# Differential attention on one core: the values' product in split form for two query tiles at once, and another order of the steps of a tile

## The chip, the cores and the metric

One Trainium2 chip, one core of it. The metric is the device time of one execution in microseconds (us), the median of the runs shown. The whole program is one launch: a hybrid layer (a state space part and forgetting attention), then a second block with differential and dilated attention, a projection and a gate. The change concerns the differential attention of the second block alone, which takes some 350 us of the 2730.

## The reference, cut to what matters

Four heads, 1024 queries and keys. Each head has two score matrices (`c`), whose softmaxes are combined with one factor `lam` and multiplied with the values of width 128.

```python
def diff_attention(q, k, v, lam, slopes):
    """q, k: (B,S,H,2,Dh) normalised; v: (B,S,H,2Dh). Returns (B,S,H,2Dh)."""
    ...
    def block(args):
        qblk, qp = args
        s = jnp.einsum('bqhce,bkhce->bchqk', qblk, k).astype(jnp.float32) * scale
        dist = jnp.abs(qp[:, None] - pos[None, :]).astype(jnp.float32)
        s = s - slopes[:, None, None] * dist
        a = jax.nn.softmax(s, axis=-1)
        w = a[:, 0] - lam * a[:, 1]
        return jnp.einsum('bhqk,bkhe->bqhe', w.astype(v.dtype), v)
```

## The kernel before

All data are float32. A product that must be accurate is made in one of two forms. The split form (`mm3`, lines 112 to 114) takes each operand as a rounded part "hi" of type fp32r and a rest "lo", and makes three matmuls: hi by hi, hi by lo, lo by hi. The plain form gives TensorE float32 operands; such a matmul stands in the trace as two records.

`diff_attend` (line 1179) works through one head in eight tiles of 128 queries. For tile i:

- **A(i)**: `scores` (line 1162) for both score matrices: four matmuls of 128x512 each into a double PSUM bank (`bank2`, two of them in all, so that one A(i) fills both), then on VectorE (DVE) a reduction that adds the distance bias and finds the minimum (line 1173, one per matrix), and on ScalarE (ACT) the exponential (line 1176), which also sums the row.
- **pre(i)**: three DVE instructions that work out the factor and combine the two matrices into one, 128x1024 (lines 1193 to 1195).
- **B(i)**: eight TensorE transposes of the combined tile (line 624), four into each of two PSUM banks (`bank`, four of them in all), and two ACT copies into the tile `pt` (line 630).
- **C(i)**: the product with the values (line 1211): eight plain matmuls of 128 columns each, 16 records, into a quarter of an output bank. After four tiles ACT copies that bank to `y`.

`pipeline` (line 523) writes the order out: A(0), A(1), and then for each i: pre(i), A(i+2), C(i-1), B(i). Engines work in the order in which their instructions are written, and wait for each other by semaphores.

`merge` puts work of the next head between these steps, by a count of estimated times and the factor `RATIOS[0]`: pieces of twelve `mm3` matmuls of the next head's k projection (called S below) and the steps of `pair_finish` for the head before. Its small sums are transposed by the lines 264 and 271, and it ends with a product over the whole head on DVE (line 1156). When the loop reaches tile 6 it gives `None`: from there on `pair_project` calls the remaining steps between its own (the `t` in `ORDERS`), which are the next head's other projections and the normalisation of q and k (`N`, with the lines 255, 264, 271 again). The values of a head, transposed to have tokens on partitions (`vtok`, line 469), are made at the end of `pair_project`.

Names below: K is the least time from the start of one tile's transposes to the start of the next tile's, if only the chain of waits counts.

Of the kernel before, what the change touches and what calls it, by code (L numbers as in the profile page):

```python
# [9 lines left out]
F32 = mybir.dt.float32  # L10
F32R = mybir.dt.float32r
BF16 = mybir.dt.bfloat16
I32 = mybir.dt.int32
AF = mybir.ActivationFunctionType
ALU = mybir.AluOpType
# [51 lines left out]
class Kern:  # L67
# [389 lines left out]
            self.nc.sync.dma_start(out=st[0][o:p, :n].bitcast(F32), in_=st[1][a:b, :n].bitcast(F32))  # L457
            self.nc.sync.dma_start(out=st[1][o:p, :n].bitcast(F32), in_=st[0][a:b, :n].bitcast(F32))

    def v_tokens(self, vT, blocks):  # L460

        nc = self.nc
        v = self.slot("vtok", w=1024)
        vv = v.rearrange("p (b c) -> p b c", c=128)
        for g in range(0, len(blocks), 4):
            ps = self.bank()
            for n, c0 in enumerate(blocks[g:g + 4]):
                nc.tensor.transpose(ps[:, n * 128:(n + 1) * 128], vT[:, c0:c0 + 128], self.ident)
            nc.scalar.activation(out=v[:, g * 128:g * 128 + 512], in_=ps, func=AF.Copy)
        return vv  # L470

    def v_meta(self, vT):

# [139 lines left out]
        yield from self.pipeline(8, A, B, C)  # L613
        nc.sync.dma_start(out=self.d_yatt[p], in_=y)

    def transposes(self, N, off, nb, pts, act=False):

        nc = self.nc
        for g in range(0, nb, 4):
            n = min(4, nb - g)  # L620
            ps = self.bank()
            for b in range(n):
                c = off + (g + b) * 128
                nc.tensor.transpose(ps[:, b * 128:(b + 1) * 128], N[:, c:c + 128], self.ident)  # L624
            self.evac(pts[g // 4][:, :n], ps[:, :n * 128].rearrange("p (b c) -> p b c", c=128), act)

    def evac(self, out, ps, act=False):
        self.ev = getattr(self, "ev", 0) + 1
# [486 lines left out]

    def v_by_tokens(self, n, st):
        vT = st.pop("vT")
        st["v"] = self.v_tokens(vT, [128 * b for b in range(8)])
        if n >= 4:
            st["vx"] = self.v_more(vT)  # L1120
            next(st["vx"])
        yield
# [56 lines left out]
    def diff_attend(self, p, st):  # L1179
        nc, te, V = self.nc, self.nc.tensor, self.nc.vector  # L1180
        y = st["y"] = self.slot("yd", w=T)
        Ws, PTs, O = {}, {}, [None]

        def A(i):
            l = self.sm.tile([128, 4], F32, tag="ld", name="ld", bufs=3)
            l0 = self.lall[:, p, i:i + 1]
            P = [self.scores(st, j, i, self.dist, DIFF_SLOPES[p], l[:, 1:2] if j else l0) for j in range(2)]
            Ws[i] = (P, l, l0)
            return 8 * 216

        def pre(i):
            P, l, l0 = Ws.pop(i)
            V.reciprocal(out=l[:, 1:2], in_=l[:, 1:2])
            V.scalar_tensor_tensor(out=l[:, 1:2], in0=l[:, 1:2], scalar=self.nlam, in1=l0, op0=ALU.mult, op1=ALU.mult)
            V.scalar_tensor_tensor(out=P[0], in0=P[1], scalar=l[:, 1:2], in1=P[0], op0=ALU.mult, op1=ALU.add)
            Ws[i] = P

        def B(i):
            P = Ws.pop(i)
            pt = self.slot("pt", w=1024)  # L1200
            r = pt.rearrange("p (b c) -> p b c", c=128)
            self.transposes(P[0], 0, 8, [r[:, :4], r[:, 4:]], act=True)
            PTs[i] = pt
            return 8 * 109

        def C(i):
            pt = PTs.pop(i)
            if i % 4 == 0:
                O[0] = self.bank()
            for b in range(8):  # L1210
                te.matmul(O[0][:, (i % 4) * 128:(i % 4 + 1) * 128], st["v"][:, b, :], pt[:, b * 128:(b + 1) * 128],
                          start=b == 0, stop=b == 7)
            if i % 4 == 3:
                nc.scalar.activation(out=y[:, (i - 3) * 128:(i + 1) * 128], in_=O[0], func=AF.Copy)
            return 8 * 218

        yield from self.pipeline(8, A, B, C, pre)

    def v_more(self, vT):

# [593 lines left out]
```

## Time and profile before

| what | us |
|---|---|
| median of 3 runs (2728.5 to 2733.69) | 2733.47 |
| the profiled execution, its own time | 2729.51 |
| its span | 2727.7 |
| TensorE (PE) busy in it | 2659.8 (98%) |
| DVE busy | 1372.3 (50%) |
| ACT busy | 1165.6 (43%) |
| GpSimd (POOL) busy | 684.5 (25%) |

The span is the time from the first to the last instruction. A matmul's record is longer than the time by which it delays the next one, since matmuls overlap in the array; so the distance from one start to the next is what a matmul costs, and a busy share of 98% says only that there is hardly a moment without one under way. A line of the timeline has the start, the duration, the engine, the line of the code, what is written from what, and in brackets how long the engine had been idle and for whom.

### The profile page before, as it was taken

The page shows a single profiled execution, that of the slowest core. Times are in us where ns is not written, and L with a number is a line of the kernel's source. Part 1 is how long each engine was busy: PE and PEld are TensorE (multiplying, and loading weights), DVE is VectorE, ACT ScalarE, POOL GpSimd, SP SyncE. Part 2 cuts the span into 40 slices and gives each one's busy share as a digit, 9 for nine tenths or more (in the row PEclk, how much of TensorE's full clock was granted, in tenths as well). Part 3 has the DMA queues.
Part 4 walks back from the last instruction along what each step waited for, and adds up shares of the span by engine and source line. Part 5 has one row for each costly group of instructions (what it writes and reads, how often), then busy time and mean ns, then how long its engine had stood idle before and what let it go on. Part 6 is the DMA issues. An engine that isn't in the chain of part 4 may idle for free. (4 is left out here: it accounts for less than half of the span.)

```text
span 2727.7 us, 38674 instructions
## 1 busy us (share of the span) xinstructions
PE 2659.8 (98%) x14925; PEld 2232.2 (82%) x14925; DVE 1372.3 (50%) x2761; ACT 1165.6 (43%) x2080; POOL 684.5 (25%) x764
## 2 busy tenths in 40 slices
PE   8999999999999999999999999999999999998999
PEld 6888888888989889889877887878877877777877
DVE  5433322233574573654756777444654555446332
ACT  5554444445343433443432123445644555445331
POOL 1112121111243342342432333111111121204321
PEclk9999999999999999999999999999999999998999
DMA  3122222221123123122168653340222223324422
GB/s 131 58 64 72 78 79 71 78 64 62 39 88 114 55 78 116 55 103 91 55 207 279 205 182 131 128 121 30 72 70 70 79 94 94 86 72 146 160 65 70
DMA packets 85464, 266.87 MB, mean 98 GB/s; under 512 B 10880, under 2 KB 12032, under 8 KB 84256
## 3 DMA queue, kind: packets, MB, share of 16 engines
q1 hardware_dynamic: 85280, 264.40, 30.3%
q8 instruction: 117, 1.92, 0.3%
q14 instruction: 67, 0.55, 0.1%
HBM read 205.57 MB, written 33.49 MB: 88 GB/s over the span
## 5 line engine op out<-in xcount | busy, mean ns | idle before, releaser
L121 POOL TENSOR_TENSOR wlo<-wraw,whi 128x1024 fp32r<-128x1024 f32 (+2 forms) x168 | 374.4, 2232 | 1288.7 <-ACT whi L120 1077.8
L112 PE MATMUL bank<-uh,whi 128*128 128x512 f32 (+4 forms) x1752 | 625.8, 357 | 0.1
L114 PE MATMUL bank<-uh,wlo 128*128 128x512 f32 (+4 forms) x1752 | 618.8, 353 | 0.1
L113 PE MATMUL bank<-ul,whi 128*128 128x512 f32 (+4 forms) x1752 | 618.5, 353 | 0.0
L114 PEld LDWEIGHTS bank<-uh,wlo 128*128 128x128 f32 (+1 forms) x1752 | 327.9, 187 | 35.4 <-POOL wlo L121 0.5
L112 PEld LDWEIGHTS bank<-uh,whi 128*128 128x128 f32 (+1 forms) x1752 | 328.3, 187 | 34.3 <-issue 1.1
L113 PEld LDWEIGHTS bank<-ul,whi 128*128 128x128 f32 (+1 forms) x1752 | 328.2, 187 | 32.3
L112 PE MATMUL bank<-u,whi 128*128 128x512 f32 x512 | 207.8, 406 | 0.7 <-ACT pr L935 0.7
L113 PE MATMUL bank<-u,whi 128*128 128x512 f32 x512 | 203.6, 398 | 0.0
L114 PE MATMUL bank<-u,wlo 128*128 128x512 f32 x512 | 203.3, 397 | 0.0
L120 ACT ACTIVATE whi<-wraw 128x1024 fp32r<-128x1024 f32 (+2 forms) x169 | 155.3, 926 | 20.5 <-DMA wraw<-in_w_pa_dram 18.2
L630 ACT ACTIVATE pt<-bank 128x512 f32<-128x512 f32 (+1 forms) x320 | 143.0, 509 | 44.8 <-PE bank L624 38.1
L114 PE MATMUL bank<-yh,wlo 128*128 128x512 f32 x384 | 152.5, 397 | 1.0 <-POOL wlo L121 0.8
L112 PE MATMUL bank<-yh,whi 128*128 128x512 f32 x384 | 152.3, 397 | 0.9 <-ACT whi L120 0.9
L113 PE MATMUL bank<-yl,whi 128*128 128x512 f32 x384 | 151.9, 395 | 0.0
L647 DVE SCALAR_TENSOR_TENSOR acc<-raw,cwh,acc 128x1040 f32<-128x1040 f32 x72 | 93.7, 1302 | 109.5 <-ACT acc L644 107.8
L573 ACT ACTIVATE N<-N,mn 128x272 f32<-128x272 f32 (+7 forms) x128 | 100.3, 786 | 45.2 <-DVE mn L570 44.0
L114 PEld LDWEIGHTS bank<-u,wlo 128*128 128x128 f32 x512 | 97.2, 190 | 23.2
L112 PEld LDWEIGHTS bank<-u,whi 128*128 128x128 f32 x512 | 97.8, 191 | 22.3 <-ACT pr L935 1.1
L113 PEld LDWEIGHTS bank<-u,whi 128*128 128x128 f32 x512 | 97.6, 191 | 20.7
L121 POOL TENSOR_TENSOR wo<-wl,wo 128x512 fp32r<-128x512 f32 x52 | 73.4, 1425 | 157.8 <-ACT wo L120 150.6
L624 PE MATMUL bank<-cm,N 128*128 128x128 f32 x832 | 106.9, 273 | 0.0
(326 smaller groups left out, 4961.5 us busy)
## 6 DMA issues: line engine op xcount, KB each, us to landing
wraw<-in_w_in_dram SPq DMA_DIRECT2D x120, 512.0 KB, 4.1
gt<-d_gate SPq DMA_DIRECT2D x48, 512.0 KB, 5.7
ab<-d_acs SPq DMA_DIRECT2D x32, 512.0 KB, 3.5
qs<-qt SPq DMA_DIRECT2D x48, 256.0 KB, 2.9
wl<-in_w_out_dram SPq DMA_DIRECT2D x48, 256.0 KB, 5.4
tab<-in_tab_dram SPq DMA_DIRECT2D x8, 1056.0 KB, 5.9
cb<-d_csp SPq DMA_DIRECT2D x16, 520.0 KB, 7.6
d_gate<-gt SPq DMA_DIRECT2D x16, 512.0 KB, 2.9
```

The lines of the kernel that those rows point to most:

```text
L112: te.matmul(ps, lh, rh, start=start, stop=False)
L113: te.matmul(ps, lh, rl, start=False, stop=False)
L114: te.matmul(ps, ll, rh, start=False, stop=stop)
L120: self.nc.scalar.activation(out=hi, in_=src, func=AF.Copy)
L121: (self.nc.vector if vector else self.nc.gpsimd).tensor_tensor(out=lo, in0=src, in1=hi.bitcast(F32), op=ALU.subtract)
L573: nc.scalar.activation(out=N[:, :W], in_=N[:, :W], func=AF.Exp, scale=-1.0, bias=mn[:, n - 1:n], accum_out=self.lall[:, 2 * p + j, i:i + 1])
L624: nc.tensor.transpose(ps[:, b * 128:(b + 1) * 128], N[:, c:c + 128], self.ident)
L630: self.nc.scalar.activation(out=out, in_=ps, func=AF.Copy)
L647: V.scalar_tensor_tensor(out=acc[:, :L], in0=raw[:, k:k + L], scalar=w(k), in1=acc[:, :L], op0=ALU.mult, op1=ALU.add)
```

## The change

The product C is made in the split form, for two tiles (256 queries) at once: 8 key blocks by 3 matmuls of 256 columns, 24 records for two tiles, where 32 stood. For this B writes hi by the ACT copy and lo by a new DVE subtraction that reads the PSUM bank and hi (two per tile), and the values get a lo of their own (two DVE subtractions per head, for the differential heads alone). The tile `pt` now holds hi and lo of both tiles of a pair, half of the keys each; it comes from a pool of its own with two buffers, so one pair fills both.

The loop is written out in place of `pipeline`: A(0), A(1), pre(0), and then for each i: B(i), A(i+2), pre(i+1), C(i-1), where C of an even tile does nothing. `None` is given ahead of B(6).

```diff
-    def v_tokens(self, vT, blocks):
+    def v_tokens(self, vT, blocks, split=False):
...
+            c = slice(g * 128, g * 128 + 512)
+            nc.scalar.activation(out=v[:, c], in_=ps, func=AF.Copy)
+            if split:
+                nc.vector.tensor_tensor(out=vs[1][:, c], in0=ps, in1=v[:, c].bitcast(F32), op=ALU.subtract)
...
+            x, hi = ps[:, :n * 128].rearrange("p (b c) -> p b c", c=128), pts[g // 4][:, :n]
+            self.evac(hi, x, act)
+            if los:
+                nc.vector.tensor_tensor(out=los[g // 4][:, :n], in0=x, in1=hi.bitcast(F32), op=ALU.subtract)
...
         def B(i):
             P = Ws.pop(i)
-            pt = self.slot("pt", w=1024)
-            r = pt.rearrange("p (b c) -> p b c", c=128)
-            self.transposes(P[0], 0, 8, [r[:, :4], r[:, 4:]], act=True)
-            PTs[i] = pt
+            if i % 2 == 0:
+                PTs[i // 2] = [self.ph.tile([128, 2, 4, 256], F32R, tag="pt", name="pt", bufs=2) for _ in range(2)]
+            q = slice((i % 2) * 128, (i % 2 + 1) * 128)
+            hi, lo = ([pt[:, x, :, q] for pt in PTs[i // 2]] for x in range(2))
+            self.transposes(P[0], 0, 8, hi, True, lo)
             return 8 * 109
 
         def C(i):
-            pt = PTs.pop(i)
-            if i % 4 == 0:
+            if i % 2 == 0:
+                return 0
+            pt, h = PTs.pop(i // 2), i // 2 % 2
+            if h == 0:
                 O[0] = self.bank()
+            o = O[0][:, h * 256:h * 256 + 256]
             for b in range(8):
-                te.matmul(O[0][:, (i % 4) * 128:(i % 4 + 1) * 128], st["v"][:, b, :], pt[:, b * 128:(b + 1) * 128],
-                          start=b == 0, stop=b == 7)
-            if i % 4 == 3:
+                hi, lo = (pt[b // 4][:, x] for x in range(2))
+                v = [x[:, b, :] for x in st["v"]]
+                self.mm3(o, v[0], v[1], hi[:, b % 4], lo[:, b % 4], b == 0, b == 7)
+            if h:
                 nc.scalar.activation(out=y[:, (i - 3) * 128:(i + 1) * 128], in_=O[0], func=AF.Copy)
-            return 8 * 218
-
-        yield from self.pipeline(8, A, B, C, pre)
+            return 8 * 357
+
+        yield A(0)
+        yield A(1)
+        pre(0)
+        for i in range(8):
+            if i == 6:
+                yield None
+            yield B(i)
+            if i + 2 < 8:
+                yield A(i + 2)
+            if i + 1 < 8:
+                pre(i + 1)
+            if i:
+                yield C(i - 1)
+        yield C(7)
```

TensorE's order in the middle of the first head, before: the transposes of tile 3 (line 624, `N_16160`), the scores of tile 6 (line 1171), the product of tile 3 (line 1211) and the transposes of tile 4.

```order
L624 MATMUL bank<-cm,N_16160 128x128 x8
L1171 MATMUL bank_16319<-qs_15924,qs_15957 128x512
L1171 MATMUL bank_16319<-qt_15925,qs_15957 128x512
L1171 MATMUL bank_16319<-qs_15924,qs_15957 128x512
L1171 MATMUL bank_16319<-qt_15925,qs_15957 128x512
L1171 MATMUL bank_16328<-qs_15926,qs_15959 128x512
L1171 MATMUL bank_16328<-qt_15927,qs_15959 128x512
L1171 MATMUL bank_16328<-qs_15926,qs_15959 128x512
L1171 MATMUL bank_16328<-qt_15927,qs_15959 128x512
L1211 MATMUL bank<-pt_16300,vtok_16034 128x128 x8
L624 MATMUL bank<-cm,N_16217 128x128 x8
```

The same place now: the transposes of tile 4 (line 629, `N_16231`), the scores of tile 6 (line 1179), and the first two matmuls of the product for the tiles 2 and 3, of 256 columns each.

```order
L629 MATMUL bank<-cm,N_16231 128x128 x8
L1179 MATMUL bank_16346<-qs_15924,qs_15957 128x512
L1179 MATMUL bank_16346<-qt_15925,qs_15957 128x512
L1179 MATMUL bank_16346<-qs_15924,qs_15957 128x512
L1179 MATMUL bank_16346<-qt_15925,qs_15957 128x512
L1179 MATMUL bank_16355<-qs_15926,qs_15959 128x512
L1179 MATMUL bank_16355<-qt_15927,qs_15959 128x512
L1179 MATMUL bank_16355<-qs_15926,qs_15959 128x512
L1179 MATMUL bank_16355<-qt_15927,qs_15959 128x512
L112 MATMUL bank<-pt,vtok_16034 128x256
L113 MATMUL bank<-pt,vtok_16034 128x256
```

The transposes of tile 4 stood behind the scores of tile 6, and stand ahead of them now; the product that follows the scores of tile 6 is that of a whole pair, and there is none behind those of tile 7.

DVE's order at the same place, before: the combination of tile 4 (`N_16217`), the two reductions of tile 6, and the combination of tile 5 (`N_16274`).

```order
L1193 RECIPROCAL ld<-ld 128x1
L1194 SCALAR_TENSOR_TENSOR ld<-ld,nlam,lall 128x1
L1195 SCALAR_TENSOR_TENSOR N_16217<-N_16226,ld,N_16217 128x1024
L1173 ISA N_16317,mn<-dist,bank_16319 128x1024
L1173 ISA mn 128x1
L1173 ISA N_16326,mn<-dist,bank_16328 128x1024
L1173 ISA mn 128x1
L1193 RECIPROCAL ld<-ld 128x1
L1194 SCALAR_TENSOR_TENSOR ld<-ld,nlam,lall 128x1
L1195 SCALAR_TENSOR_TENSOR N_16274<-N_16283,ld,N_16274 128x1024
```

And now: the same instructions with new line numbers (`N_16231` is tile 4, `N_16306` tile 5), and the subtractions of line 633, two for tile 4 and two for tile 5.

```order
L1203 SCALAR_TENSOR_TENSOR N_16231<-N_16240,ld,N_16231 128x1024
L633 TENSOR_TENSOR pt<-bank,pt 128x4x128 x2
L1181 ISA N_16344,mn<-dist,bank_16346 128x1024
L1181 ISA mn 128x1
L1181 ISA N_16353,mn<-dist,bank_16355 128x1024
L1181 ISA mn 128x1
L1201 RECIPROCAL ld<-ld 128x1
L1202 SCALAR_TENSOR_TENSOR ld<-ld,nlam,lall 128x1
L1203 SCALAR_TENSOR_TENSOR N_16306<-N_16315,ld,N_16306 128x1024
L633 TENSOR_TENSOR pt<-bank,pt 128x4x128 x2
```

On DVE nothing has changed its place; the two subtractions of a tile have come between its combination and the reductions of the tile two further on.

## Rows read from the trace of the kernel before

**Rows 1.** The page: span, TensorE's busy time, its granted clock by slices.

```profile
span 2727.7 us, 38674 instructions
PE 2659.8 (98%) x14925; PEld 2232.2 (82%) x14925; DVE 1372.3 (50%) x2761; ACT 1165.6 (43%) x2080; POOL 684.5 (25%) x764
PEclk9999999999999999999999999999999999998999
```

**Rows 2.** Busy time by engine in the differential stage (us, busy, records, clock, DMA).

```profile
1834.00:2182.00 348.00, 338.14 (x1874) 277.48 (x1873) 186.90 (x336) 182.25 (x301) 49.59 (x54) 1.00 0.23 66
```

**Rows 3.** Timeline of TensorE in the second head, tiles without work between.

```profile
1959.13 0.48 PE L1171 MATMUL bank<-qs,qs 128*128 128x512 f32 x1
...
1961.08 1.95 PE L1211 MATMUL bank<-pt,vtok 128*128 128x128 f32 x16
1962.86 1.04 PE L624 MATMUL bank<-cm,N 128*128 128x128 f32 x8
1963.65 0.48 PE L1171 MATMUL bank<-qs,qs 128*128 128x512 f32 x1
...
1964.68 0.39 PE L1171 MATMUL bank<-qs,qs 128*128 128x512 f32 x1
```

**Rows 4.** Timeline of DVE there: two reductions and a combination.

```profile
1964.88 1.22 DVE L1173 CUSTOM_DVE_ANT_0 N<-dist,bank 128x1024 f32<-128x1024 f32 x1 [0.52 <-PE bank L1171]
...
1967.17 0.16 DVE L1193 RECIPROCAL ld<-ld 128x1 f32<-128x1 f32 x1
...
1967.62 1.28 DVE L1195 SCALAR_TENSOR_TENSOR N<-N,ld,N 128x1024 f32<-128x1024 f32 x1
```

**Rows 5.** Timeline of ACT there: the two copies of a tile's transposes.

```profile
1959.49 1.06 ACT L630 ACTIVATE pt<-bank 128x512 f32<-128x512 f32 x2
```

**Rows 6.** DVE groups by shape: operations from a PSUM bank and SBUF, 128x512.

```profile
L520 DVE SCALAR_TENSOR_TENSOR zs<-zs,bank 128x512 f32<-128x512 f32 x32 | 21.6, 685 | 85.7 <-ACT zs L519 85.6
L903 DVE SCALAR_TENSOR_TENSOR gt<-gt,bank 128x512 f32<-128x512 f32 x80 | 54.4, 680 | 22.6 <-PE bank L114 22.5
```

**Rows 7.** Timeline of all engines at the start of the first head.

```profile
1841.83 0.39 PE L1171 MATMUL bank<-qs,qs 128*128 128x512 f32 x1
...
1844.11 0.08 DVE L1173 DVE_READ_ACCUMULATOR2_ANT mn<- 128x1 f32 x1
...
1844.24 0.50 PE L1171 MATMUL bank<-qs,qs 128*128 128x512 f32 x1 [0.38 <-DVE mn L1173]
...
1846.45 0.40 PE L112 MATMUL bank<-u,whi 128*128 128x512 f32 x1
...
1849.23 1.04 PE L624 MATMUL bank<-cm,N 128*128 128x128 f32 x8
```

**Rows 8.** TensorE's waits in the stage (us in total, times, longest).

```profile
PE bank L271 <- DVE rsv L246: 4.4, 3, 1.5
PE bank L271 <- POOL lall L1145: 2.7, 3, 0.9
PE bank L1267 <- DVE zs L520: 2.0, 1, 2.0
```

**Rows 9.** Timeline of DVE in the second head: line 1156 ahead of a combination.

```profile
1950.79 1.22 DVE L1156 TENSOR_TENSOR yd<-yd,rb 128x1024 f32<-128x1024 f32 x1
1951.92 0.16 DVE L1193 RECIPROCAL ld<-ld 128x1 f32<-128x1 f32 x1
```

**Rows 10.** Timeline of matmuls and weight loads in split form, 272 columns.

```profile
21.75 0.29 PE L112 MATMUL bank<-uh,whi 128*128 128x272 f32 x1
...
23.64 0.29 PE L112 MATMUL bank<-uh,whi 128*128 128x272 f32 x1
...
21.76 0.19 PEld L113 LDWEIGHTS bank<-ul,whi 128*128 128x128 f32 x1
21.88 0.19 PEld L114 LDWEIGHTS bank<-uh,wlo 128*128 128x128 f32 x1
```

**Rows 11.** Stretches behind the stage (columns as in group 2; the clock ahead of DMA).

```profile
2191.00:2194.50 3.50, 1.46 (x12) 1.11 (x11) 3.28 (x3) 2.94 (x5) 2.42 (x1) 1.00 0.45 98
2194.60:2197.90 3.30, 2.97 (x10) 2.52 (x10) 1.69 (x7) 0.96 (x2) 3.29 (x16) 0.50 0.99 330
2198.00:2201.00 3.00, 3.00 (x14) 1.92 (x14) 0.41 (x2) 1.91 (x3) 1.47 (x3) 1.00 0.08 29
2491.60:2498.30 6.70, 6.00 (x33) 5.09 (x34) 3.77 (x15) 2.41 (x6) 3.96 (x4) 0.50 0.67 238
```

More of the change, by code (lines that the diff above doesn't have):

```diff
@@ L458, in move_k @@
             self.nc.sync.dma_start(out=st[1][o:p, :n].bitcast(F32), in_=st[0][a:b, :n].bitcast(F32))
-    def v_tokens(self, vT, blocks):
+    def v_tokens(self, vT, blocks, split=False):
         nc = self.nc
-        v = self.slot("vtok", w=1024)
-        vv = v.rearrange("p (b c) -> p b c", c=128)
+        vs = [self.slot("vtok", F32R if split else F32, 1024) for _ in range(1 + split)]
+        v = vs[0]
         for g in range(0, len(blocks), 4):
@@ L468, in v_tokens @@
                 nc.tensor.transpose(ps[:, n * 128:(n + 1) * 128], vT[:, c0:c0 + 128], self.ident)
-            nc.scalar.activation(out=v[:, g * 128:g * 128 + 512], in_=ps, func=AF.Copy)
-        return vv
+            c = slice(g * 128, g * 128 + 512)
+            nc.scalar.activation(out=v[:, c], in_=ps, func=AF.Copy)
+            if split:
+                nc.vector.tensor_tensor(out=vs[1][:, c], in0=ps, in1=v[:, c].bitcast(F32), op=ALU.subtract)
+        vs = [x.rearrange("p (b c) -> p b c", c=128) for x in vs]
+        return vs if split else vs[0]
     def v_meta(self, vT):
@@ L614, in fox_attend, with transposes @@
         nc.sync.dma_start(out=self.d_yatt[p], in_=y)
-    def transposes(self, N, off, nb, pts, act=False):
+    def transposes(self, N, off, nb, pts, act=False, los=None):
         nc = self.nc
@@ L624, in transposes @@
                 nc.tensor.transpose(ps[:, b * 128:(b + 1) * 128], N[:, c:c + 128], self.ident)
-            self.evac(pts[g // 4][:, :n], ps[:, :n * 128].rearrange("p (b c) -> p b c", c=128), act)
+            x, hi = ps[:, :n * 128].rearrange("p (b c) -> p b c", c=128), pts[g // 4][:, :n]
+            self.evac(hi, x, act)
+            if los:
+                nc.vector.tensor_tensor(out=los[g // 4][:, :n], in0=x, in1=hi.bitcast(F32), op=ALU.subtract)
     def evac(self, out, ps, act=False):
@@ L1117, in v_by_tokens @@
         vT = st.pop("vT")
-        st["v"] = self.v_tokens(vT, [128 * b for b in range(8)])
+        st["v"] = self.v_tokens(vT, [128 * b for b in range(8)], n < 4)
         if n >= 4:
```

## The prediction

> **What bounds the kernel now.** I read the page first, then the stage's sums, then the timeline of single tiles. The page shows TensorE busy nearly all the time, and its clock granted in full but for one slice [rows 1]; in the differential stage too it is busy 338 of 348 us, while DVE and ACT have some 185 us of work each [rows 2]. In the timeline the reader is to see that TensorE goes from tile to tile without a break: scores from 1959.13 to 1961.08 (1.95 us), product to 1962.86 (1.78), transposes to 1963.65 (0.79), so 4.52 us a tile [rows 3]. DVE needs two reductions, 2.29 us from the first's start at 1964.88 to the reciprocal at 1967.17, and 1.73 more until the combination ends at 1967.62 + 1.28 = 1968.90 [rows 4]: about 4.0 us a tile. TensorE is the bound, but DVE is close behind, and the chain from one to the other is long. What keeps it harmless is the order: between the scores whose reductions end a combination's wait and that tile's transposes stand the scores of a further tile and a product.
>
> **What the product saves.** Plain form: 1.78 us a tile, 3.57 a pair [rows 3]. Split form with 256 columns has no row; the nearest has 272: from 21.75 to 23.64 there are 15 matmuls, 0.126 us each [rows 10], which for 256 columns is 0.119 by length (0.126 if length did not count), so 24 make 2.84 us (3.02). Saved: 0.73 us a pair, 16 pairs, **11.7 us** (8.8 at the other end). Here a rule speaks against the change: a load of weights could fail to hide behind the matmul in front. In these rows each matmul has a load of its own, recorded as 0.19 us [rows 10], and still they start 0.126 apart; were loads and matmuls to take turns, a pair would take 24 x (0.19 + 0.119) = 7.4 us. The Trainium skill, "TensorE: Matmul & The Clock Gate", section "The mechanism", says that a load overlaps running matmuls only where it goes to another group of rows, and these go to the same; by its section "LDWEIGHTS (loading the stationary operand)" a load of 128 columns takes 107 ns, and a pair would then take, as an estimate, 24 x (0.107 + 0.107) = 5.1 us. I follow the row.
>
> **What DVE gets.** Two subtractions from a bank a tile: 0.68 us each [rows 6], 0.62 when one follows another (the overlap of 0.07 that the combination shows). The shape is that of the rows, so I take it as it stands. 64 of them are 40 us, and the eight for the values 5 us more. The latter cost nothing: they only delay the first reductions of a head, and the first combination waits for the second tile's reductions anyway, a stretch of TensorE work later; without that cover, 1.2 us a head. The ACT copies remain 64, no DMA is issued or moved, and POOL's and SP's queues hold what they held.
>
> **What the order costs.** B(i) now stands ahead of A(i+2), so B(i+1) follows A(i+2) directly or with one piece between, and its combination is queued on DVE behind the two subtractions of tile i and the reductions of tile i+2. K, from the start of B(i): four transposes 0.44, 0.20 until the next engine starts (the second matrix's first matmul starts at 1964.68, so the first matrix's are issued, and DVE starts on them at 1964.88 [rows 3, 4]), two copies 1.06 [rows 5], which brings the second subtraction's start to 1.83 behind the first; its 0.62 to 2.45; reductions 2.29, combination 1.73, 0.05 back to TensorE (DVE's 1844.11 + 0.08 to 1844.24 [rows 7]): **K = 6.5 us**. TensorE's own work from B(i) to B(i+1) is 0.79 + 1.95 = 2.74, plus a piece S of 2.78 where there is one (1846.45 to 1849.23 [rows 7]), plus 2.84 for a product.
>
> By the order of the first head, TensorE waits:
> - ahead of B(0) and of B(1): the scores in front of each follow a piece S, so from their start half of them 0.93, then 0.20 + 2.29 + 1.73 + 0.05 = 5.2 us, less the 1.86 of the scores: 3.3 each;
> - ahead of B(2), with S between: 6.5 - 5.5 = 1.0;
> - ahead of B(4), with nothing between but A(5): 6.5 - 2.7 = 3.8.
>
> **The buffers.** B(2) writes the next pair's `pt`, and both buffers are held by the pair whose product C(1) stands behind A(4) on TensorE. So ACT's copies of B(2) wait for that product, and behind them on DVE the subtractions, the reductions of tile 4 and the combination of tile 3, for which B(3) waits. From the product's start: its second half frees the second buffer at 2.84, + 0.20, copy 0.57, subtraction 0.62, reductions 2.29, combination 1.73, 0.05 = 8.3 us, less the product itself 2.84: TensorE waits 5.5 us ahead of B(3), and the same ahead of B(5). For B(6) the wait is hidden by the projection that `pair_project` puts there, 24 matmuls (5.6 us).
>
> A head then waits 3.3 + 3.3 + 1.0 + 5.5 + 3.8 + 5.5 = 22.4 us; in the other three line 1156 comes ahead of the combination of tile 3 with 1.13 us [rows 9], 23.5. Four heads: **93.0 us**. What goes: the wait where A(2) followed A(1), 1841.83 to 1846.45 being 4.62 us for 3.72 of scores, 0.9 a head [rows 7], and the waits of line 271 for POOL, 2.7 in three heads [rows 8], covered by the longer stops: -6.3. What comes behind the loop: line 271's wait for DVE (4.4 in three heads [rows 8]) grows, since the transposes of tile 7 no longer stand between 264 and 271 (0.8) and the subtractions of tile 7 stand ahead of its DVE work (1.2): +2.0 in three heads and 0.8 in the last, +6.8.
>
> Sum without the clock: 93.0 - 6.3 + 6.8 - 11.7 = **+81.8 us**.
>
> **The clock.** Now the clock is full in the stage [rows 2], where the longest stop is 1.5 us [rows 8]. Behind the stage line 1267 waits 2.0 us [rows 8], until 2194.4, and from 2194.6 for 3.3 us the clock is 0.50, that is 1.2 GHz of 2.4, and full again at 2198; one stretch at half clock is 6.7 us long [rows 11]. The new order has 20 stops of 3.3 us and more in the loops and 3 of about 3.5 behind them. A stretch of 3.4 us at half clock delays TensorE by 1.7; if each stop brings one, 39 us. Some of that falls into the stops themselves, or on work that the chain of waits does not pass through. With no row for stops so long I take half, 19 us, and keep 0 and 39 as bounds.
>
> **Sum:** 81.8 + 19 = 101 us on the profiled execution's 2729.5: **2830 us**. The median of the runs shown is 4 us above that execution; a difference of 0.2%, some 5 us, is about what can be told from no change.
>
> **The rivals.**
> 1. The stops cost no clock: 2729.5 + 81.8 = 2811. For it: stops of 2 us behind the stage do not all show in the page's slices [rows 1]. Against: [rows 11].
> 2. Every stop costs the full 1.7, or longer stretches: 2811 + 39 = 2850 and above.
> 3. The buffers do not bind, as the product frees them early enough. Then ahead of B(3) TensorE has 2.74 + 2.78 + 2.84 = 8.4 of work for a K of 6.5, no wait, and ahead of B(5) 6.5 - 5.6 = 0.9: four heads lose 4 x (5.5 + 4.6) + 3.4 = 44 less, so 2767, with some clock 2780. Against it: the pool has two buffers and a pair takes both.
> 4. TensorE stays the bound, and the product's gain is all that counts: 2729.5 - 11.7 = 2718, faster. This needs K below TensorE's mean of 2.74 + 1.42 = 4.2 us a tile, thus reductions and subtractions that cost some 2.3 us less than their rows, or overlap of neighbouring tiles that DVE's order rules out. For it: DVE's mean load in the stage, 187 of 348 us [rows 2], leaves room for 45 more.
> 5. Loads and matmuls take turns: 16 x (7.4 - 2.84) = 73 us more than the sum, less what vanishes in the stops that a longer product shortens, around 2880. The Trainium skill's rule above would bring this; the trace disagrees at 272 columns [rows 10].
>
> **How the numbers follow.** Chances: forecast 0.50, rival 1 0.25, rival 2 0.12, rival 3 0.06, rival 4 0.04, rival 5 0.03. The first three are one mechanism with the clock's price open: 2811 to 2850, and some 15 us on either side for K, of which each 0.2 us moves 24 waits by 5 us: 2795 to 2865. That leaves out the rivals 3 to 5 and the far end of 2. Slower 0.95, same 0.01, faster 0.04.
>
> **What the profile after would show.** TensorE's waits headed by the transposes (line 629) waiting for DVE's combination (line 1203), 24 of them, the longest near 5.5 us ahead of the odd tiles 3 and 5; ACT's copies into `pt` of tiles 2 and 4 waiting for the product; matmuls of 256 columns some 0.119 us apart; the stage some 100 us longer, and half clock in it. The prediction is wrong if the transposes wait for nothing, if the copies of tile 2 run before the product of the first pair, or if DVE's subtractions take far less or more than 0.68 us.

## The result, and the profile after

| what | before | after |
|---|---|---|
| median, us | 2732.98 (2728.5 to 2733.69) | 2852.39 (2849.97 to 2855.56) |
| ratio, 95% interval | | 1.0444 (1.0433 to 1.0455) |
| the profiled execution, its own time | 2729.51 | 2851.41 |

Six runs of each kernel. The change makes the kernel 4.4% slower; the profiled execution is 121.9 us longer. The page of after, with the rows that answer to [rows 1], and two groups of instructions (busy time and mean ns of one, then the idle time of the engine in front of them and what ended it):

```profile
span 2849.6 us, 38478 instructions
PE 2689.1 (94%) x14797; PEld 2250.5 (79%) x14797; DVE 1418.8 (50%) x2833; ACT 1171.5 (41%) x2080; POOL 680.7 (24%) x764
PEclk9999999999999999999999999989889899999999
L629 PE MATMUL bank<-cm,N 128*128 128x128 f32 x832 | 123.1, 299 | 87.5 <-DVE N L1203 87.5
L633 DVE TENSOR_TENSOR pt<-bank,pt 128x512 fp32r<-128x512 f32 x64 | 43.7, 690 | 147.9 <-ACT pt L638 147.9
```

TensorE is recorded as busy for 29 us longer than before, although it has 128 matmuls fewer: its records are longer at half clock (one of 512 columns lasts 0.63 us there, and 0.39 at full clock). The transposes (line 629) now have 87.5 us of idle time in front of them, all ended by the combination (line 1203). TensorE's waits in the differential stage say the same, beside [rows 8]:

```profile
PE bank L629 <- DVE N L1203: 87.5, 24, 6.6
PE bank L271 <- DVE rsv L246: 7.7, 3, 2.6
PE bank L112 <- DVE pt L633: 1.6, 3, 0.5
PE bank L264 <- ACT sums L257: 1.2, 1, 1.2
```

The waits for POOL are gone. The stage and two pieces of it (columns as in [rows 2], the clock ahead of the DMA share):

```profile
1834.00:2304.00 470.00, 371.10 (x1740) 298.68 (x1739) 233.79 (x408) 187.84 (x302) 46.89 (x54) 0.88 0.17 49
1846.00:1853.00 7.00, 5.97 (x18) 5.08 (x19) 2.35 (x3) 1.79 (x4) 0.00 (x0) 0.52 0.00 0
1877.00:1883.50 6.50, 3.16 (x12) 2.90 (x13) 4.37 (x9) 4.55 (x8) 0.00 (x0) 0.50 0.01 3
```

Where the granted clock of the whole stage was 1.00, it is 0.88, so half clock (1.2 GHz) held for (1 - 0.88) x 2 x 470 = 113 us. The two pieces lie around the stops ahead of B(0) and B(3) of the first head, each about twice as long at half clock as the 3.4 us that I had assumed.

One stop in full, ahead of B(3) of the first head. TensorE's timeline: the product of the first pair, and the transposes of tiles 3 and 4.

```profile
1871.84 0.28 PE L112 MATMUL bank<-pt,vtok 128*128 128x256 f32 x1
...
1874.57 0.28 PE L114 MATMUL bank<-pt,vtok 128*128 128x256 f32 x1
1880.34 1.94 PE L629 MATMUL bank<-cm,N 128*128 128x128 f32 x8 [5.49 <-DVE N L1203]
...
1888.16 1.94 PE L629 MATMUL bank<-cm,N 128*128 128x128 f32 x8 [3.27 <-DVE N L1203]
```

ACT's timeline there: the copies of tile 2.

```profile
1873.52 0.60 ACT L638 ACTIVATE pt<-bank 128x512 fp32r<-128x512 f32 x1 [7.77 <-PE bank L114]
1874.95 0.60 ACT L638 ACTIVATE pt<-bank 128x512 fp32r<-128x512 f32 x1 [0.83 <-PE bank L114]
```

DVE's timeline there: tile 2's subtractions, tile 4's reductions, tile 3's combination.

```profile
1874.15 0.69 DVE L633 TENSOR_TENSOR pt<-bank,pt 128x512 fp32r<-128x512 f32 x1 [8.03 <-ACT pt L638]
1875.58 0.69 DVE L633 TENSOR_TENSOR pt<-bank,pt 128x512 fp32r<-128x512 f32 x1 [0.73 <-ACT pt L638]
1876.19 1.21 DVE L1181 CUSTOM_DVE_ANT_0 N<-dist,bank 128x1024 f32<-128x1024 f32 x1
...
1878.46 0.16 DVE L1201 RECIPROCAL ld<-ld 128x1 f32<-128x1 f32 x1
...
1878.91 1.28 DVE L1203 SCALAR_TENSOR_TENSOR N<-N,ld,N 128x1024 f32<-128x1024 f32 x1
```

Follow one chain through these rows. The copies of tile 2, whose transposes are long done, start only when the product has read half of `pt` (1873.52) and all of it (1874.95). DVE has waited 8.03 us for the first of them. Behind it come, without a gap worth speaking of, the subtractions, the reductions of tile 4 and the combination of tile 3, which ends at 1880.19; TensorE starts at 1880.34. From the product's start that is 8.50 us; I had worked out 8.3.

### The profile page after: what moved, and what is told of

Its sections match the earlier page's. It is cut to its first block, busy times and chain, and to the rows that moved or that the text cites. A ratio compares the mean times of both kernels' runs of the same rounds, so it can differ in the third digit from the quotient of the medians.

```text
span 2849.6 us, 38478 instructions
## 1 busy us (share of the span) xinstructions
PE 2689.1 (94%) x14797; PEld 2250.5 (79%) x14797; DVE 1418.8 (50%) x2833; ACT 1171.5 (41%) x2080; POOL 680.7 (24%) x764
## 5 line engine op out<-in xcount | busy, mean ns | idle before, releaser
L629 PE MATMUL bank<-cm,N 128*128 128x128 f32 x832 | 123.1, 299 | 87.5 <-DVE N L1203 87.5
L638 ACT ACTIVATE pt<-bank 128x512 f32<-128x512 f32 (+2 forms) x320 | 146.3, 510 | 122.5 <-PE bank L114 72.5
L629 PEld LDWEIGHTS bank<-cm,N 128*128 128x128 f32 x832 | 104.3, 155 | 100.4 <-issue 41.4
L112 PEld LDWEIGHTS bank<-u,whi 128*128 128x128 f32 x512 | 99.9, 195 | 25.3 <-DVE pt L633 2.3
L633 DVE TENSOR_TENSOR pt<-bank,pt 128x512 fp32r<-128x512 f32 x64 | 43.7, 690 | 147.9 <-ACT pt L638 147.9
```

The source lines that it names most:

```text
L112: te.matmul(ps, lh, rh, start=start, stop=False)
L633: nc.vector.tensor_tensor(out=los[g // 4][:, :n], in0=x, in1=hi.bitcast(F32), op=ALU.subtract)
L638: self.nc.scalar.activation(out=out, in_=ps, func=AF.Copy)
```

## The experiments

Each ran beside the kernel before on the same chip; the ratio is to that. "Split" is the changed kernel's product; "the new order" its loop. Dots stand for lines of code, or of a view, that are not shown.

**One part of the change at a time.** First the split product in the old order of steps:

```diff
-        yield A(0)
-        yield A(1)
-        pre(0)
-        for i in range(8):
...
-        yield C(7)
+        yield from self.pipeline(8, A, B, C, pre)
```

> The split product for two tiles is kept, the order of the steps is that of the kernel before. If the order makes the waits (my theory), the transposes no longer follow directly on the scores whose reductions stand ahead of their combination, and the first product stands ahead of the copies that need its buffers: the stops of 5.5 us go, and the clock stays full. DVE then takes 5.2 us a tile (reductions 2.29, combination 1.66, subtractions 1.24) where TensorE takes 4.2 without other work, so part of the product's 11.7 us is eaten: 2730 us, between 2720 and 2740. If the subtractions of the split form are the cause in whatever order, above 2800.

Measured: 2776.23 us (2769.07 to 2778.77), ratio 1.0163 (1.0148 to 1.0178). I was wrong: with the old order the split product is slower too. TensorE's longest wait in the stage is that of the transposes again:

```profile
PE bank L629 <- DVE N L1203: 24.3, 9, 4.0
```

ACT's timeline in the first head: two exponentials, then a tile's copies.

```profile
1871.48 1.15 ACT L1184 ACTIVATE N<-N,mn 128x1024 f32<-128x1024 f32 x1 [3.65 <-DVE mn L1181]
1872.63 1.14 ACT L1184 ACTIVATE N<-N,mn 128x1024 f32<-128x1024 f32 x1
1873.77 1.06 ACT L638 ACTIVATE pt<-bank 128x512 fp32r<-128x512 f32 x2
```

DVE's timeline there: a tile's subtractions ahead of the next combination, and the next tile's.

```profile
1874.37 1.29 DVE L633 TENSOR_TENSOR pt<-bank,pt 128x512 fp32r<-128x512 f32 x2 [1.79 <-ACT pt L638]
1876.02 1.28 DVE L1203 SCALAR_TENSOR_TENSOR N<-N,ld,N 128x1024 f32<-128x1024 f32 x1
...
1881.87 1.29 DVE L633 TENSOR_TENSOR pt<-bank,pt 128x512 fp32r<-128x512 f32 x2 [2.28 <-ACT pt L638]
```

In the old order the scores of tile i+2 stand ahead of the transposes of tile i, so on ACT the copies stand behind that tile's exponentials, 2.3 us. The subtraction needs the copy's hi, and so DVE waits (1.79 us, 2.28) where before it had nothing to do with the copies. From one pair of subtractions to the next are 7.5 us. By these rows it is the subtraction that ties DVE, ACT and TensorE into one ring; no run has the split product without it in the old order. The clock has its part in the loss too: it is 0.95 over 386 us of the stage. Then the new order with the plain product of the kernel before:

```diff
-        yield from self.pipeline(8, A, B, C, pre)
+        yield A(0)
+        yield A(1)
+        pre(0)
+        for i in range(8):
+            if i == 6:
+                yield None
+            yield B(i)
+            if i + 2 < 8:
+                yield A(i + 2)
+            if i + 1 < 8:
+                pre(i + 1)
+            if i:
+                yield C(i - 1)
+        yield C(7)
```

> The kernel before with the new order of the steps alone, the product in the plain form. If the order makes the waits: 3.3 us ahead of tiles 0 and 1, 1.6 ahead of a tile with no other work between, some 40 us in four heads, and 10 us of half clock: 2780 us. If the split form with its subtractions is what costs: 2733, as before.

Measured: 2783.94 us (2782.82 to 2787.72), ratio 1.0198 (1.0183 to 1.0213), as expected. TensorE's timeline in the first head, the transposes of tiles 0, 1, 3 and 4:

```profile
1849.02 1.06 PE L624 MATMUL bank<-cm,N 128*128 128x128 f32 x8 [3.27 <-DVE N L1195]
1857.91 1.97 PE L624 MATMUL bank<-cm,N 128*128 128x128 f32 x8 [3.17 <-DVE N L1195]
...
1875.64 1.07 PE L624 MATMUL bank<-cm,N 128*128 128x128 f32 x8 [1.48 <-DVE N L1195]
1881.85 1.07 PE L624 MATMUL bank<-cm,N 128*128 128x128 f32 x8 [1.48 <-DVE N L1195]
```

The stops of 3.3 us ahead of the first two tiles belong to the order; the 5.5 and 3.3 us ahead of tiles 3 and 4 shrink to 1.48 without the subtractions and without pairs of buffers. Either part alone costs 1.6 to 2.0%, the two together 4.4%.

**The buffers.** Even pairs as in the change, odd pairs in four tiles of another pool, so that two pairs fit:

```diff
-                PTs[i // 2] = [self.ph.tile([128, 2, 4, 256], F32R, tag="pt", name="pt", bufs=2) for _ in range(2)]
+                if i % 4 == 0:
+                    PTs[i // 2] = [self.ph.tile([128, 2, 4, 256], F32R, tag="pt", name="pt", bufs=2) for _ in range(2)]
+                else:
+                    PTs[i // 2] = [[self.slot("pt", F32R, 1024).rearrange("p (b c) -> p b c", c=256)
+                                    for _ in range(2)] for _ in range(2)]
...
```

> As the changed kernel, but every second pair's hi and lo lie in other buffers, so that ACT's copies of tiles 2 and 4 needn't wait for the product of the pair before. If the buffers bind, the stops ahead of tiles 3 and 5 shrink from 5.5 us to 0 and 0.9, that is 44 us in four heads, and 14 us more of half clock go with them: 2794 us. If the buffers don't bind, no change from 2852.

Measured: 2804.07 us (2803.51 to 2806.26), ratio 1.0271 (1.0255 to 1.0286). The buffers bind: 48 us of the loss go with them, what the clock takes included. TensorE's timeline in the first head, the transposes of tiles 3 to 5:

```profile
1876.97 1.03 PE L629 MATMUL bank<-cm,N 128*128 128x128 f32 x8
1883.60 1.94 PE L629 MATMUL bank<-cm,N 128*128 128x128 f32 x8 [3.73 <-DVE N L1203]
1891.92 1.09 PE L629 MATMUL bank<-cm,N 128*128 128x128 f32 x8
```

Here the stops ahead of tiles 3 and 5 are gone; that ahead of tile 4, which I had put down to K, stays with 3.73 us. In the other three heads 2.3 us are left ahead of tile 3; there DVE has the product over a whole head (line 1156 of the kernel before) ahead of the combination. These three are most of the 10 us by which I was too low. Next, what the buffers delay: this kernel leaves out the tiles' subtractions, and its product reads hi in place of lo.

```diff
-            self.transposes(P[0], 0, 8, hi, True, lo)
+            self.transposes(P[0], 0, 8, hi, True)
...
-                hi, lo = (pt[b // 4][:, x] for x in range(2))
+                hi = lo = pt[b // 4][:, 0]
```

> As the changed kernel, but the tiles' subtractions are left out: the product takes hi in the place of lo, so that its result is not the split one. TensorE's work is the same. If the wait for the buffers reaches the transposes through the subtractions (DVE stands behind ACT's late copies), the stops ahead of tiles 3 and 5 go: 2775 us. If the buffers hold up TensorE in another way, through ACT's exponentials, those stops stay, and only some 1 us a tile goes: above 2810.

Measured: 2785.86 us (2782.66 to 2792.76), ratio 1.0197 (1.0182 to 1.0213). TensorE's timeline, the transposes of tiles 3 and 5:

```profile
1879.39 0.60 PE L629 MATMUL bank<-cm,N 128*128 128x128 f32 x4
1880.30 0.65 PE L629 MATMUL bank<-cm,N 128*128 128x128 f32 x4 [0.31 <-ACT pt L638]
...
1892.21 1.09 PE L629 MATMUL bank<-cm,N 128*128 128x128 f32 x8 [0.43 <-DVE N L1203]
```

ACT's timeline there, the first copy of tile 2:

```profile
1878.28 0.60 ACT L638 ACTIVATE pt<-bank 128x512 fp32r<-128x512 f32 x1 [7.76 <-PE bank L114]
```

The copies still wait for the product, but the combination doesn't: the wait for a buffer reaches TensorE through DVE's subtractions, not by way of ACT's exponentials. That is the path of the forecast.

**The clock.** Ahead of each tile's transposes come 12, 12, 0, 20, 13, 20 extra matmuls of 512 columns (none for the last two tiles). They write the same bank, which the transposes then overwrite.

```diff
...
             ps = self.bank()
+            if g == 0:
+                for x, y in fill:
+                    nc.tensor.matmul(ps, x, y, start=True, stop=True)
...
-            self.transposes(P[0], 0, 8, hi, True, lo)
+            k = st["k"][0][0]
+            self.transposes(P[0], 0, 8, hi, True, lo, [(k[:, :128], k[:, :512])] * (12, 12, 0, 20, 13, 20, 0, 0)[i])
```

> As the changed kernel, but TensorE fills most of each stop ahead of tiles 0, 1, 3, 4 and 5 with matmuls whose result the transposes overwrite (12, 12, 20, 13 and 20 of 512 columns, 2.8 to 4.6 us, each less than its stop). They add work and change no result. If the half clock behind the stops costs some 40 us, as the difference of the measured 119 and the 82 of the waits says, it goes: 2811 us, with a clock near 1.0 in the stage. If the clock costs nothing, since the chain of waits sets the end anyway, 2852 or a little more.

Measured: 2821.58 us (2820.53 to 2826.09), ratio 1.0336 (1.0319 to 1.0354). The stage (with 13 us behind it), and the piece ahead of B(0) and behind it, by windows; then the wait of the transposes behind the extra matmuls, and TensorE's timeline with the transposes of tiles 3 and 4 of the first head:

```profile
1834.00:2300.00 466.00, 429.51 (x2176) 343.46 (x2175) 252.52 (x447) 205.20 (x328) 56.34 (x74) 0.99 0.20 57
1846.00:1853.00 7.00, 6.56 (x33) 5.23 (x32) 4.68 (x9) 4.33 (x7) 2.43 (x1) 1.00 0.00 0
```

```profile
PE bank L631 <- DVE N L1205: 19.9, 25, 1.6
```

```profile
1880.53 1.09 PE L631 MATMUL bank<-cm,N 128*128 128x128 f32 x8 [0.52 <-DVE N L1205]
...
1887.13 1.09 PE L631 MATMUL bank<-cm,N 128*128 128x128 f32 x8 [0.68 <-DVE N L1205]
```

With 308 matmuls of needless work the kernel is faster, since the clock stays at 0.99 in the stage and at 1.00 where it was 0.52. The transposes still wait behind the extra matmuls, at least 0.4 us in each of the filled stops, so these made no stop longer. The difference of the two ratios, 0.0108 of 2731, is 29 us, give or take 6 by their intervals. The traces can be compared over the stage alone, from its first scores to the first matmul of the stage behind it: 357.3 us before (1837.12 to 2194.41), 480.7 after (1836.59 to 2317.24), 446.1 here (1840.47 to 2286.52). By that the change costs 123 us in the stage, and the half clock 35 of them. What stays is waiting without it: 91 us by the medians, 89 by the stage.

**Other places for the combination.** The chain as I saw it suggests moving `pre(i + 1)` ahead of A(i+2), so that DVE combines before it reduces:

```diff
-            if i + 2 < 8:
-                yield A(i + 2)
             if i + 1 < 8:
                 pre(i + 1)
+            if i + 2 < 8:
+                yield A(i + 2)
```

> As the changed kernel, but the combination of tile i+1 is written ahead of the scores of tile i+2, so that it stands on DVE ahead of their reductions. If the combination's place behind the reductions is what makes the transposes wait, the 2.3 us of reductions leave the chain: no wait ahead of tiles 1 and 2, 3.2 in place of 5.5 ahead of tiles 3 and 5, some 2.7 ahead of tile 4, 3.3 ahead of tile 0 as before; 40 us less in four heads and 10 less of half clock: 2800 us. If DVE's total work is the bound, its place changes nothing: 2852.

Measured: 2813.27 us (2810.93 to 2818.51), ratio 1.0301 (1.0285 to 1.0316). The first head's tiles 3, 4 and 5:

```profile
1872.02 1.06 PE L629 MATMUL bank<-cm,N 128*128 128x128 f32 x8 [3.21 <-DVE N L1203]
1879.99 1.79 PE L629 MATMUL bank<-cm,N 128*128 128x128 f32 x8 [3.25 <-DVE N L1203]
1890.49 1.97 PE L629 MATMUL bank<-cm,N 128*128 128x128 f32 x8 [3.12 <-DVE N L1203]
```

The stop ahead of tile 3 falls by the 2.3 us of the reductions, from 5.49 to 3.21, so the reductions did stand in that chain. That ahead of tile 4 stays, where I had expected 2.7; this is a part of the 13 us by which I was too low. With the buffers of `e2_more_buffers` as well, and `pre(0)` ahead of A(1):

```diff
         yield A(0)
-        yield A(1)
         pre(0)
+        yield A(1)
```

> The same, with the further buffers for every second pair, and the first tile's combination ahead of the second tile's scores. If the two causes are the order and the buffers, the stops are gone but for DVE's own load, some 5.4 us a tile against TensorE's 4.2 where no other work lies between: 3 to 5 us a head, and the clock near full: 2737 us, between 2725 and 2750. If something else keeps TensorE waiting, above 2760.

Measured: 2760.91 us (2760.44 to 2762.84), ratio 1.0104 (1.009 to 1.0118): above the range I gave. TensorE still waits for the combination 13 times, 22.6 us. ACT's timeline in the first head:

```profile
1871.78 1.14 ACT L1184 ACTIVATE N<-N,mn 128x1024 f32<-128x1024 f32 x1
1872.91 0.57 ACT L1049 ACTIVATE qraw<-bank 128x512 f32<-128x512 f32 x1
...
1873.87 1.07 ACT L638 ACTIVATE pt<-bank 128x512 fp32r<-128x512 f32 x2
```

DVE's timeline there:

```profile
1874.49 1.29 DVE L633 TENSOR_TENSOR pt<-bank,pt 128x512 fp32r<-128x512 f32 x2 [2.82 <-ACT pt L638]
```

It is the ring of `e1_old_order` again: copies behind exponentials (here of tile i+1, and a projection's copy), subtractions behind copies, the next combination behind the subtractions. So I gave the ring a tile more of room, with the buffers as above: three tiles of scores ahead, two combinations ahead (and a fourth buffer for `ld`).

```diff
...
         yield A(0)
         yield A(1)
         pre(0)
+        yield A(2)
+        pre(1)
         for i in range(8):
...
             yield B(i)
+            if i + 3 < 8:
+                yield A(i + 3)
             if i + 2 < 8:
-                yield A(i + 2)
-            if i + 1 < 8:
-                pre(i + 1)
+                pre(i + 2)
```

> The further buffers, and scores three tiles ahead of the transposes, so that a tile's combination is done a whole tile before its transposes. No transposes wait for their combination then; if DVE's load (5.2 us a tile against 4.2 on TensorE) is all that is left, some 4 us a head: 2735 us, between 2722 and 2750. If the depth doesn't matter, as with the combination first, within 5 us of that kernel.

Measured: 2738.46 us (2735.28 to 2741.44), ratio 1.0022 (1.0013 to 1.0031). The waits for the combination are gone but for two of 0.2 us. What is left at the end of a head was tested in that kernel by ending the step between tiles 6 and 7 earlier, so that B(7) stands behind line 264 again, as it did before:

```diff
+            if i == 7:
+                yield C(6)
             yield B(i)
...
-            if i:
+            if 0 < i < 7:
                 yield C(i - 1)
```

> As the kernel with scores three tiles ahead, and the empty step of tile 6 is given ahead of the transposes of tile 7, so that these stand again behind line 264's transposes and hide line 271's wait. If the 1.8 us a head that this place costs are as read from the trace of the changed kernel, 5 to 6 us less in four heads: 2733 us, the same as before. If line 271's wait is set by something else, no change from 2738.

Measured: 2733.16 us (2729.79 to 2734.54), ratio 1.0003 (0.9995 to 1.0012): no difference from the kernel before. The stage by windows, over the stretch of [rows 2], and TensorE's two largest waits in it:

```profile
1834.00:2182.00 348.00, 332.26 (x1749) 266.15 (x1748) 237.64 (x409) 180.68 (x303) 46.62 (x54) 1.00 0.23 67
```

```profile
PE bank L271 <- DVE pt L633: 6.0, 3, 2.0
PE bank L1179 <- DVE mn L1181: 5.5, 8, 1.1
```

The second of them in the kernel before:

```profile
PE bank L1171 <- DVE mn L1173: 1.6, 4, 0.4
```

TensorE is recorded as busy 5.9 us less in the same stretch, and DVE 50.7 us more: a part of the product's gain shows there, and waits take all of it back. The scores' wait for DVE's minima, 5.5 us where it was 1.6, has grown most. Line 271, which now waits for the subtractions, waits no longer than before (6.2 us in all, 7.7 before); the rest lies in waits that come to some 2 us and less by line. From one tile's subtractions to the next DVE now needs 1.29 + 2.27 + 1.73 = 5.3 us by the rows above, where TensorE has 4.2 of its own between inserted pieces. Last, in the same kernel, DVE's load: the combination of odd tiles on GpSimd, as a product and a sum.

```diff
-            V.scalar_tensor_tensor(out=P[0], in0=P[1], scalar=l[:, 1:2], in1=P[0], op0=ALU.mult, op1=ALU.add)
+            if i % 2:
+                nc.gpsimd.tensor_scalar(out=P[1], in0=P[1], scalar1=l[:, 1:2], scalar2=None, op0=ALU.mult)
+                nc.gpsimd.tensor_tensor(out=P[0], in0=P[0], in1=P[1], op=ALU.add)
+            else:
+                V.scalar_tensor_tensor(out=P[0], in0=P[1], scalar=l[:, 1:2], in1=P[0], op0=ALU.mult, op1=ALU.add)
```

> The same, and the combination of every odd tile is made on GpSimd in two instructions (a product and a sum, each of 128x1024, nearest row 2.4 us), which takes 1.28 us off DVE for every second tile. If DVE's load is what still makes TensorE wait (1 to 3 us a head), the split product's gain comes through: 2726 us, faster than before. If GpSimd is too late for the transposes, or slows DVE down, 2735 to 2760.

Measured: 2762.41 us (2758.83 to 2765.21), ratio 1.0113 (1.0098 to 1.0129). GpSimd's groups and TensorE's wait:

```profile
L1204 POOL TENSOR_SCALAR N<-N,ld 128x1024 f32<-128x1024 f32 x15 | 42.8, 2853 | 73.4 <-DVE ld L1202 41.3 <-ACT N L1184 32.1
L1205 POOL TENSOR_TENSOR N<-N,N 128x1024 f32<-128x1024 f32 x15 | 37.3, 2489 | 1.3
```

```profile
PE bank L629 <- POOL N L1205: 20.6, 9, 4.3
```

It takes 5.3 us where DVE takes 1.3, and TensorE waits for it. No kernel of the study beats the kernel before.

## Why the prediction was right, and where it was off

The forecast was 2830 us in a range of 2795 to 2865; measured were 2852. Mechanism and sign were right; the clock was put too low, and the waiting a little. So the number is nearer to the 2850 of rival 2 (chance 0.12) than to the forecast.

- **The product, -11.7.** Confirmed. 23 distances of the first pair's product take 1874.57 - 1871.84 = 2.73 us, 0.119 each. Every one of these matmuls has a weight load of its own, recorded as 0.19 us as in [rows 10], so rival 5 falls at 256 columns too. The rule of the Trainium skill, "TensorE: Matmul & The Clock Gate", section "The mechanism", that a load overlaps only with matmuls in another group of rows, does not hold for this product.
- **The subtraction, 0.68.** 0.69 measured.
- **The stops ahead of the transposes, +93.0.** With the stops filled and a full clock (`e4_filled_stops`) they come out tile by tile. A stop is here the time from the start of the last matmul of the kernel's own work (the extra ones left out) to the start of the transposes, less the 0.23 or 0.12 that this matmul takes. The first head has 3.3 us ahead of B(0), 3.3 ahead of B(1), 1.1 ahead of B(2) (forecast 1.0), 5.6 ahead of B(3) (5.5), 3.8 ahead of B(4) (3.8) and 5.6 ahead of B(5) (5.5). The four heads have 94.3. K is 1887.13 - 1880.53 = 6.6 (forecast 6.5, in whose sum the terms named up to the second subtraction make 1.70 and not 1.83). In the trace after, slower work fills some of the same stops: 0.4 ahead of B(2), 3.4 ahead of B(4). There 24 waits are on record, as said, but one of those foretold, ahead of B(2) of the third head, is missing, and one of 1.3 us ahead of B(7) of the last head had not been foreseen.
- **The cause of the stops.** The buffers bind (`e2_more_buffers`: rival 3 falls), through the subtractions (`e7_no_subtractions`), with the reductions in the same chain (`e5_combine_first`).
- **What goes and what comes at the heads' ends, -6.3 and +6.8.** The sum of the two was right to 1 us, its parts were not. TensorE's other waits in the stage come to 11.3 us where they were 9.9. Line 271's wait is 7.7 as before and did not grow; line 112 waits 1.6 us for the subtractions of the last tile, and line 264 waits 1.2, neither of which I had listed.
- **The sum without the clock, +81.8.** Measured are 89 to 91 (`e4_filled_stops`). Of the 7 us that the stage has more, 1.3 lie in the stops foretold, 1.5 in the one ahead of B(7) and 1 at the heads' ends. The other 3 stay open; a part may be half clock, which that run still has for some 9 us (0.99 over 466).
- **The clock, +19.** The term that was mis-sized most: "a stretch of 3.4 us at half clock" per stop, and half of 39 taken. It costs 29 us by the medians and 35 by the stage. Half clock held for 113 us, 4.9 per stop over 23 stops, where I had 3.4. With the stops filled, 9 us of it were left, so each microsecond of the others cost 29 / (113 - 9) = 0.28, or 0.33 by the stage. A microsecond at half clock can cost 0.5 at most, and taking half of that was not far off, as a part fell on the stops themselves (the second piece of the windows after shows one); the length of the stretches was. The bounds 0 and 39 hold the price. The stage is 123.4 us longer, where the forecast was 101: the clock is 16 of the 22 missing ones by this measure, the waiting 7.
- **Rival 4**, that TensorE stays the bound, was excluded with the right reason, but my thought behind it was too narrow: I took the new order for the cause. `e1_old_order` shows that the split product with its subtractions takes the slack out of the old order too, which my expectation of 2730 missed.

## What to carry to other kernels

An engine at half load can still set the pace. Ask of each added instruction which queue it joins, what stands ahead of it there and who waits behind it: the subtraction cost 0.6 us of DVE, but it made DVE wait for ACT's copies, and with them for exponentials and for buffers. When the unit of work doubled here (a pair for a tile), the buffers had to double too, and the steps had to run a tile further ahead, before the loss was gone. A saving on TensorE that buys work on an engine with 4.0 us a tile against TensorE's 4.5 may be worth nothing: here it took two more buffers and another order to be at par.

## What the runs showed of the hardware that I had not expected

- Stops of TensorE of 3 to 7 us cost more than themselves: in this stage the clock fell to half on such stops, for 113 us in all, and that took 29 us (medians) to 35 us (the stage's trace) beyond the waiting. Filling the stops with 308 matmuls whose result is overwritten brought those back.
- GpSimd needs 2.85 us for a product of 128x1024 with a factor per row and 2.49 us for a sum of two tiles, where DVE does both in one instruction of 1.29 us.
